# Second branch's output projection: the last pair of heads last for three feature tiles, two of them held behind the last head's values, the fourth on a score bank

## The chip, the cores and the metric

The kernel runs on one core of a Trainium2 chip. The time is that of one execution on the device, in microseconds; the median of several runs counts. The engines are TensorE (PE, matrix products, with its weight loads PEld), VectorE (DVE), ScalarE (ACT), GpSimd (POOL) and SyncE (SP, which issues most DMAs). Each works through its own instructions in the order of its program; waits between engines are semaphores. Products land in PSUM, eight banks of 128 x 512 float32.

## What is computed

One layer of an encoder over 512 frames of width 1024, in float32:

```python
hn = rms_norm(x, norm1_g[l])
proj = hn @ w_in[l]                       # q, k, v of branches A and B, gates A and B
out_a = chunked_attention(qa, ka, va, ...)      # 8 heads x 64, softmax
out_b = stick_breaking_attention(qb, kb, vb)    # 8 heads x 64, no softmax
mixed = (sigmoid(gate_a) * (out_a @ w_branch_a[l])
         + sigmoid(gate_b) * (out_b @ w_branch_b[l]))
x = x + mixed @ w_out[l]
x = x + conv_glu(rms_norm(x, norm2_g[l]), ...)
```

The change concerns `out_b @ w_branch_b[l]`, a product of 512 x 512 by 512 x 1024.

## The kernel before

Every float32 product is made of three: both operands are split into a rounded high part and the rest (`hi`, `lo`), and `mm3` issues high by high (L312), high by rest (L313) and rest by high (L314) into one bank. A step of the contraction (128 wide) is thus three products, each with a stationary 128 x 128 block and 512 moving columns. In `mm3` for the second branch the stationary operand is the weight (`whi_yB`, `wlo_yB`) and the moving one the heads' output (`oh_B`, `ol_B`).

The weights come in chunks in a fixed order; the ones here are `gB3` (gates), `yB0` and `yB1` (the two halves of `w_branch_b`, four feature tiles each) and `wo0` to `wo3`. `run_chunk` runs a chunk's body, and between the body's yields it emits the casts of the next chunk (`split_gen`: L281 on ACT for the high part, L286 on DVE for the rest).

The attention heads run in steps. For the last head of branch B, `trans` transposes the weights of the attention (L770) and splits them (L783 on ACT into `pth_B`, L784 on DVE into `ptl_B`), and `pv` multiplies them with the values (L793, eight products, 512, 384, 256 and 128 columns wide, each for `pth` and `ptl`). Its result is put together over ACT (L800, `ot_B`) and DVE (L801, `of_B`) and split again: `oh_B` (L805, ACT) and `ol_B` (L806, DVE). Two heads make one pair, 128 rows; `ots["B"]` holds the four pairs, and the contraction of the output projection runs over them, `k` 0 to 3. Pair 3 is complete only after the last head's `pv`.

`yB_body` uses `feat_groups`: for each feature tile one bank, and in it the four pairs in order. The evacuation of a tile multiplies by the gate (`gb`, L882), adds to the first branch's part (`mixA`, L883), and splits into `mh` (L889, ACT) and `ml` (L890, DVE). After each tile the loop around it emits two pieces of `park`, background work that has nothing to do with this stage: blocks of the later up-projection are summed (`pkr`, L203, DVE), split (L208 ACT, L209 DVE) and stored by DMA.

What is written is an order of emission. A planner then orders each engine's instructions: it takes ready instructions by priority, by its own model of costs, and hands out buffers from the pools; `tc.high_priority` raises the priority (as around `trans` and `pv`), and `park` lowers it. An emission order is thus a wish and not the final one; `behind(ins, others)` adds an order between two instructions without a semaphore. On chip each engine's order is fixed.

The PSUM banks are handed out by tag:

```python
SC = lambda n: ptile("sc", 2, n)     # two banks, scores
TR = lambda n: ptile("tr", 2, n)     # two banks, transposes
PV = lambda n: ptile("pv", 1, n)     # one bank, attention times values
MM = lambda n: ptile("mm", 3, n)     # three banks, projections
```

and the loops that use them here are

```python
def feat_groups(hi, lo, name, n, kn, mh, ml, evac):
    for j in range(n):
        ps = MM(f"{name}_{j}")
        for k in range(kn):
            cs = slice(j * P, (j + 1) * P)
            mm3(ps, hi[:, k, cs], lo[:, k, cs], mh(k), ml(k), k == 0, k == kn - 1)
```

After yB1 the output projection `wo` takes its banks in turn from SC, TR, PV and MM.

Of the kernel before, what the change touches and what calls it, by code (L numbers as in the profile page):

```python
# [15 lines left out]
P = 128  # L16
S = 512
D = 1024
NT = S // P
# [56 lines left out]
def block_kernel(ctx: ExitStack, tc: tile.TileContext, x, xt, params, g2, rbx, wts, wd0, wd1, out):  # L76
    nc = tc.nc
    V, A, G, PE, SP = nc.vector, nc.scalar, nc.gpsimd, nc.tensor, nc.sync
# [230 lines left out]

    def mm3(ps, sh, sl, mh, ml, first, last):  # L310

        PE.matmul(ps, sh, mh, start=first, stop=False)  # L312
        PE.matmul(ps, sh, ml, start=False, stop=False)  # L313
        PE.matmul(ps, sl, mh, start=False, stop=last)  # L314


    hth = hp.tile([P, NK, S], F32R, tag="hth", name="hth")
# [15 lines left out]
    def ptile(tag, bufs, name):  # L333
        return pp.tile([P, S], F32, tag=tag, name=name, bufs=bufs)

    SC = lambda n: ptile("sc", 2, n)
    TR = lambda n: ptile("tr", 2, n)
    PV = lambda n: ptile("pv", 1, n)
    MM = lambda n: ptile("mm", 3, n)
# [21 lines left out]
    for i in range(WARM):  # L361
        PE.matmul(pw.rearrange("p (a b) -> p a b", a=4), warm, warm.unsqueeze(1).to_broadcast([P, 4, P]),
                  start=True, stop=True)
# [139 lines left out]
    def tok_groups(hi, lo, name, evac):  # L503
        for tp in range(2):
            ps = MM(f"{name}_{tp}")
            for j in range(2):
                t = 2 * tp + j
                o = ps[:, j * 256:(j + 1) * 256]
                for k in range(NK):
                    ts_ = slice(t * P, (t + 1) * P)  # L510
                    mm3(o, hth[:, k, ts_], htl[:, k, ts_], hi[:, k, :], lo[:, k, :], k == 0, k == NK - 1)
                if j == 1:
                    evac(tp, ps)
                yield
# [78 lines left out]
# [6 lines that stand above are left out]
                if kn == 8 and k == 3:  # L599
                    yield  # L600
            evac(j, ps)
            yield
# [131 lines left out]
    def behind(ins, others):  # L734

        for o in others:
            tc.add_manual_dep(ins.ins, o.ins.name, mybir.DependencyInfo(
                mybir.DependencyClass.NoSync, mybir.DependencyReason.DATA), reason="table order")
        return ins
# [46 lines left out]
    def pv(br, h):  # L786
        ph, pl = pts.pop((br, h))
        vt = vts[f"v{br}{h // 4}"]
        ps = PV(f"pv_{br}{h}")
        for k in range(NT):  # L790
            o, n = OFF[k] + k * P, S - k * P
            for j, src in enumerate((ph, pl)):
                PE.matmul(ps[:, k * P:], vt[:, k, h % 4, :], src[:, o:o + n],  # L793
                          start=(k == 0 and j == 0), stop=(k == NT - 1 and j == 1))
        i = h % 2
        if i == 0:
            pv.o = pool_o.tile([P, S], F32, tag="of", name=f"of_{br}{h}", bufs=1)
        tmp = pool_wk.tile([P, S], F32, tag="wb", name=f"ot_{br}{h}", bufs=5)
        own, oth = ((LO, HI), (HI, LO))[i]
        A.copy(tmp[own, :], ps[oth, :])  # L800
        V.tensor_tensor(pv.o[own, :], ps[own, :], tmp[own, :], op=ALU.add)  # L801
        if i == 1:
            oh = pool_o.tile([P, S], F32R, tag="oh", name=f"oh_{br}{h}", bufs=4)
            ol = pool_o.tile([P, S], F32R, tag="ol", name=f"ol_{br}{h}", bufs=4)
            A.copy(oh, pv.o)  # L805
            V.tensor_tensor(ol, pv.o, oh.bitcast(F32), op=ALU.subtract)  # L806
            ots[br].append((oh, ol))
# [44 lines left out]
    for s in range(len(steps)):  # L852
        if s + LA < len(steps):
            start_step(s + LA)
        target = n_groups * (s + 1) / (len(steps) + 6)
        while emitted < target:
            next(fg, None)
            emitted += 1
        if 14 <= s < 56:
            park()  # L860
        br, h, t, e = pend.pop(0)
        with tc.high_priority(HP):
            trans(br, h, t, e)
        if t == NT - 1:
            if (br, h) in need_v:
                fill_until(need_v[br, h])
            with tc.high_priority(HP):
                pv(br, h)
# [5 lines left out]
    def yB_body(i):  # L874
        def body(hi, lo):
            o = ots["B"]
            m = mix["t"]

            def evac(j, ps):
                f = 4 * i + j  # L880
                g = gbs[f]
                V.tensor_tensor(g, ps, g, op=ALU.mult)  # L882
                V.tensor_tensor(m[:, f, :], g, m[:, f, :], op=ALU.add)  # L883
                if f % 4 == 0:
                    mxt["h"] = pool_v.tile([P, 4, S], F32R, tag="v", name=f"mh{f}", bufs=2)
                if f % 2 == 0:
                    mxt["l"] = pool_pt.tile([P, 2, S], F32R, tag=("pth", "ptl")[f // 2 % 2], name=f"ml{f}", bufs=2)
                mh, ml = mxt["h"][:, f % 4, :], mxt["l"][:, f % 2, :]
                A.copy(mh, m[:, f, :])  # L889
                V.tensor_tensor(ml, m[:, f, :], mh.bitcast(F32), op=ALU.subtract)  # L890
                mxs.append((mh, ml))
            yield from feat_groups(hi, lo, f"yB{i}", 4, 4, lambda k: o[k][0], lambda k: o[k][1], evac)
        return body

    n = 0
# [22 lines left out]
    def rows_group(prefix, banks, src, n, fin, c, t, hi, lo):  # L918

        for hf in range(2):  # L920
            if c == 0:
                banks[t, hf] = BANK(f"{prefix}_{t}{hf}", t // 2)
            ps = banks[t, hf]
            for kk in range(2):
                sh, sl = src[2 * c + kk]
                ts_, cs = slice(t * P, (t + 1) * P), slice(hf * 512, (hf + 1) * 512)
                mm3(ps, sh[:, ts_], sl[:, ts_], hi[:, kk, cs], lo[:, kk, cs],
                    c == 0 and kk == 0, c == n - 1 and kk == 1)
            if c == n - 1:
                fin(t, hf, ps)  # L930
            yield
# [31 lines left out]
    hi, lo = splits.pop("wo3")  # L963
# [448 lines left out]
```

## Time and profile before

| | us |
|---|---|
| median of 3 runs (range) | 720.12 (719.87 to 720.14) |
| the profiled execution | 719.62 |
| its span, first to last instruction | 717.9 |
| PE busy | 711.6 |
| DVE busy | 588.6 |
| ACT busy | 410.0 |
| POOL busy | 55.2 |
| granted TensorE clock, mean | 1.00 |

Times in the trace count from the start of the span. The stage of the change lies at about 309 to 328 us. In a timeline a row is the start, the duration, the engine, the line, the operation, output and inputs by tile name (buffer numbers left out), and in brackets the idle time ahead of it and what ended it; in the list of waits the three numbers are the total, the number of times and the longest. In a row by stretches the engines' busy times stand behind the stretch's length, then the granted clock and the DMA figures.

### The profile page before, as it was taken

The page shows a single profiled execution, that of the slowest core. Times are in us where ns is not written, and L with a number is a line of the kernel's source. Part 1 is how long each engine was busy: PE and PEld are TensorE (multiplying, and loading weights), DVE is VectorE, ACT ScalarE, POOL GpSimd, SP SyncE. Part 2 cuts the span into 40 slices and gives each one's busy share as a digit, 9 for nine tenths or more (in the row PEclk, how much of TensorE's full clock was granted, in tenths as well). Part 3 has the DMA queues.
Part 4 walks back from the last instruction along what each step waited for, and adds up shares of the span by engine and source line. Part 5 has one row for each costly group of instructions (what it writes and reads, how often), then busy time and mean ns, then how long its engine had stood idle before and what let it go on. Part 6 is the DMA issues. An engine that isn't in the chain of part 4 may idle for free.

```text
span 717.9 us, 10814 instructions
## 1 busy us (share of the span) xinstructions
PE 711.6 (99%) x3983; PEld 619.6 (86%) x3983; DVE 588.6 (82%) x1051; ACT 410.0 (57%) x756; POOL 55.2 (8%) x91
## 2 busy tenths in 40 slices
PE   9999999999999999999999999999999999999997
PEld 7889998888988888878889988999988988888886
DVE  6678878786998998869556698999999985997687
ACT  6576657667776677544335564656655543543531
POOL 2501200000110111100003000000000100000000
PEclk9999999999999999999999999999999999999999
DMA  9722236435344444554937837667665633564563
GB/s 315 290 75 89 89 118 204 164 132 205 137 162 142 180 159 159 199 184 162 336 127 284 270 112 280 231 235 284 246 249 205 230 132 113 187 247 167 179 213 117
DMA packets 38613, 136.59 MB, mean 190 GB/s; under 512 B 4128, under 2 KB 8864, under 8 KB 31008
## 3 DMA queue, kind: packets, MB, share of 16 engines
q1 hardware_dynamic: 35616, 122.66, 47.9%
q0 software_dynamic: 2656, 13.11, 4.9%
q8 instruction: 31, 0.51, 0.3%
q14 instruction: 22, 0.18, 0.1%
q10 hardware_dynamic: 288, 0.14, 0.1%
HBM read 109.41 MB, written 26.48 MB: 189 GB/s over the span
## 4 chain that ended last, share of the span: by engine, by line
PE 97%; DVE 2%; ACT 0%; issue 0%; DVEq 0%; ACTq 0%
PE P L1245 15%; PE p L1151 12%; PE pg L313 3%; PE pg L312 3%; PE pg L314 3%; PE pu L313 3%; PE pu L314 3%; PE pu L312 3%; PE vA L443 3%; PE uA L443 3%; PE qkB L314 2%; PE gB L312 2%; PE qkB L312 2%; PE qkB L313 2%; PE gB L313 2%; PE gB L314 2%
## 5 line engine op out<-in xcount | busy, mean ns | idle before, releaser
L1245 PE MATMUL P<-whi_dn,ax 128*128 128x512 f32 x176 | 54.3, 389 | 0.0
L166 ACT CAST whi_dn<-raw_dn 128x1024 fp32r<-128x1024 f32 x33 | 34.3, 1051 | 25.8 <-PE P L1245 16.5
L162 DVE TENSOR_TENSOR wlo_dn<-raw_dn,whi_dn 128x1024 fp32r<-128x1024 f32 x33 | 40.0, 1223 | 9.5 <-ACT whi_dn L166 9.5
L314 PE MATMUL pg<-hth,wlo_up 128*128 128x512 f32 (+1 forms) x120 | 43.3, 361 | 0.0
L312 PE MATMUL pg<-hth,whi_up 128*128 128x512 f32 (+1 forms) x120 | 43.2, 361 | 0.0
L313 PE MATMUL pg<-htl,whi_up 128*128 128x512 f32 (+1 forms) x120 | 43.2, 360 | 0.0
L313 PE MATMUL pu<-htl,whi_up 128*128 128x512 f32 (+1 forms) x116 | 41.6, 359 | 0.0
L312 PE MATMUL pu<-hth,whi_up 128*128 128x512 f32 (+1 forms) x116 | 41.6, 359 | 0.0
L314 PE MATMUL pu<-hth,wlo_up 128*128 128x512 f32 (+1 forms) x116 | 41.6, 358 | 0.0
L1245 PE MATMUL P<-whi_dn,ay 128*128 128x512 f32 x132 | 40.8, 389 | 0.0
L1245 PEld LDWEIGHTS P<-whi_dn,ax 128*128 128x128 f32 x176 | 33.0, 188 | 6.8
L208 ACT CAST pkh<-pkr 128x512 fp32r<-128x512 f32 x24 | 14.9, 621 | 36.5 <-DMA parked<-pkh 15.3
L286 DVE TENSOR_TENSOR wlo_up<-raw_up,whi_up 128x1024 fp32r<-128x1024 f32 (+1 forms) x32 | 31.3, 1019 | 4.9 <-ACT whi_up L281 4.9
L1245 PE MATMUL P<-wlo_dn,ax 128*128 128x512 f32 x88 | 34.2, 389 | 0.0
L281 ACT CAST whi_up<-raw_up 128x1024 fp32r<-128x1024 f32 (+1 forms) x32 | 26.5, 886 | 10.9 <-PE pu L313 6.1
L754 POOL TENSOR_SCALAR_AFFINE_SELECT bB<-bB 128x128 f32<-128x128 f32 x32 | 18.7, 592 | 151.4 <-DVE bB L753 149.3
L1245 PEld LDWEIGHTS P<-whi_dn,ay 128*128 128x128 f32 x132 | 24.8, 188 | 5.1
L752 DVE TENSOR_TENSOR_SCAN aB<-aB,reset 128x127 f32<-128x127 f32 (+3 forms) x32 | 25.7, 813 | 4.1 <-ACT aB L747 4.1
L209 DVE TENSOR_TENSOR pkr<-pkr,pkh 128x512 fp32r<-128x512 f32 x24 | 16.4, 684 | 12.4 <-ACT pkh L208 12.4
L1245 PE MATMUL P<-wlo_dn,ay 128*128 128x512 f32 x66 | 25.8, 391 | 0.0
L312 PE MATMUL gA<-hth,whi_gA 128*128 128x512 f32 x64 | 25.5, 399 | 0.3 <-DVE mixA L632 0.3
L1151 PE MATMUL p<-ts,whi_up 128*128 128x256 f32 x144 | 25.5, 277 | 0.0
(324 smaller groups left out, 2397.6 us busy)
## 6 DMA issues: line engine op xcount, KB each, us to landing
raw_up<-in_wts SPq DMA_DIRECT2D x14, 1024.0 KB, 5.4
raw_dn<-in_wd SPq DMA_DIRECT2D x11, 1024.0 KB, 4.8
pkr<-in_wts SPq DMA_DIRECT2D x8, 1024.0 KB, 6.8
parked<-pkr SPq DMA_DIRECT2D x32, 256.0 KB, 2.5
parked<-pkh SPq DMA_DIRECT2D x24, 256.0 KB, 2.1
raw_dn<-in_wd SPq DMA_DIRECT2D x11, 512.0 KB, 3.3
ayd<-ay POOLq DMA_DIRECT2D x7, 768.0 KB, 6.3
ay<-ayd POOLq DMA_DIRECT2D x7, 768.0 KB, 6.1
```

Of the source, the lines that this page charges most:

```text
L162: chain("halves", V.tensor_tensor(o, x, y, op=op))
L166: chain("casts", A.copy(hi[:, sl], src))
L281: A.copy(hi[:, sl], raw[:, sl])
L286: V.tensor_tensor(lo[:, sl], raw[:, sl], hi[:, sl].bitcast(F32), op=ALU.subtract)
L312: PE.matmul(ps, sh, mh, start=first, stop=False)
L313: PE.matmul(ps, sh, ml, start=False, stop=False)
L314: PE.matmul(ps, sl, mh, start=False, stop=last)
L443: PE.matmul(pss[t], st[:, 4 * half + k, t * P:(t + 1) * P], mv[:, k, :], start=half == 0 and k == 0 and j == 0, stop=half == 1 and k == 3 ...
L752: V.tensor_tensor_scan(ar, ar, reset[:, S - n:S - 1][:, ::-1], 1.0, op0=ALU.mult, op1=ALU.max)
L754: G.affine_select(b[:, n - P:n], b[:, n - P:n], pattern=[[-1, P]], compare_op=ALU.is_gt, fill=0.0, base=0, channel_multiplier=1)
L1151: PE.matmul(ps, st, mv[:, k, :], start=first and k == 0 and n == 0, stop=last and k == 3 and n == 2, skip_group_check=True)
L1245: chain("products", PE.matmul(dst, st, mv, start=first and n == 0, stop=last and n == 2, skip_group_check=True))
```

## The change

`mm3` returns its first instruction, and `pv` keeps its last one. For `yB0` the loop is written out: three tiles take MM banks; for each the first three pairs are emitted, then for each the last pair with the evacuation; then the fourth tile in one piece, on an SC bank. The first products of tiles 1 and 2 are ordered behind the last product of `pv`. `yB1` is as before. The yields stay four, one behind each tile's evacuation.

```diff
     def mm3(ps, sh, sl, mh, ml, first, last):
 
-        PE.matmul(ps, sh, mh, start=first, stop=False)
+        ins = PE.matmul(ps, sh, mh, start=first, stop=False)
         PE.matmul(ps, sh, ml, start=False, stop=False)
         PE.matmul(ps, sl, mh, start=False, stop=last)
+        return ins
...
             for j, src in enumerate((ph, pl)):
-                PE.matmul(ps[:, k * P:], vt[:, k, h % 4, :], src[:, o:o + n],
-                          start=(k == 0 and j == 0), stop=(k == NT - 1 and j == 1))
+                pv.last = [PE.matmul(ps[:, k * P:], vt[:, k, h % 4, :], src[:, o:o + n],
+                                     start=(k == 0 and j == 0), stop=(k == NT - 1 and j == 1))]
...
-            yield from feat_groups(hi, lo, f"yB{i}", 4, 4, lambda k: o[k][0], lambda k: o[k][1], evac)
+            if i == 1:
+                yield from feat_groups(hi, lo, "yB1", 4, 4, lambda k: o[k][0], lambda k: o[k][1], evac)
+                return
+            pss = [MM(f"yB0_{j}") for j in range(3)]
+            for j, ks in [(j, (0, 1, 2)) for j in range(3)] + [(j, (3,)) for j in range(3)] + [(3, range(4))]:
+                if j == 3:
+                    pss.append(SC("yB0_3"))
+                cs = slice(j * P, (j + 1) * P)
+                for k in ks:
+                    ins = mm3(pss[j], hi[:, k, cs], lo[:, k, cs], *o[k], k == 0, k == 3)
+                    if k == 0 and j in (1, 2):
+                        behind(ins, pv.last)
+                if 3 in ks:
+                    evac(j, pss[j])
+                    yield
```

## The prediction

> **What bounds the kernel now.** First the page, for the shares of the engines and the chain that ended last; then the list of waits of TensorE; then the timeline around the second branch's output projection.
>
> ```profile
> span 717.9 us, 10814 instructions
> PE 711.6 (99%) x3983; PEld 619.6 (86%) x3983; DVE 588.6 (82%) x1051; ACT 410.0 (57%) x756; POOL 55.2 (8%) x91
> PE 97%; DVE 2%; ACT 0%; issue 0%; DVEq 0%; ACTq 0%
> ```
>
> TensorE (PE) is busy for 99% of the span and makes up 97% of the chain that ended last. So time can be won only where PE stands still or steps slowly. The list of waits, for PE alone and over the whole span, has four entries:
>
> ```profile
> PE warm L362 <- DVE warm L359: 1.1, 1, 1.1
> PE yB L313 <- DVE ol_B L806: 0.4, 1, 0.4
> PE gA L312 <- DVE mixA L632: 0.3, 1, 0.3
> PE yB L312 <- DVE gb L882: 0.3, 1, 0.3
> ```
>
> Two of the four lie in yB, the tile that the change touches. PE's timeline there:
>
> ```profile
> 306.94 0.60 PE L770 MATMUL pT_B<-ident,bB 128*128 128x128 f32 x4
> ...
> 309.00 0.39 PE L312 MATMUL yB<-oh_B,whi_yB 128*128 128x512 f32 x1
> ...
> 312.42 0.39 PE L793 MATMUL pv_B<-pth_B,v_vB 128*128 128x512 f32 x1
> 312.64 0.39 PE L312 MATMUL yB<-oh_B,whi_yB 128*128 128x512 f32 x1
> ...
> 313.10 0.39 PE L793 MATMUL pv_B<-ptl_B,v_vB 128*128 128x512 f32 x1
> ...
> 314.08 0.44 PE L314 MATMUL yB<-oh_B,wlo_yB 128*128 128x512 f32 x1
> 314.36 0.39 PE L312 MATMUL yB<-oh_B,whi_yB 128*128 128x512 f32 x1
> ...
> 316.43 0.89 PE L312 MATMUL yB<-oh_B,whi_yB 128*128 128x512 f32 x3
> 317.75 0.50 PE L313 MATMUL yB<-ol_B,whi_yB 128*128 128x512 f32 x1 [0.43 <-DVE ol_B L806]
> 318.09 0.39 PE L314 MATMUL yB<-oh_B,wlo_yB 128*128 128x512 f32 x1
> ...
> 319.01 0.40 PE L314 MATMUL yB<-oh_B,wlo_yB 128*128 128x512 f32 x1
> 319.67 0.50 PE L312 MATMUL yB<-oh_B,whi_yB 128*128 128x512 f32 x1 [0.26 <-DVE gb L882]
> 320.01 0.40 PE L313 MATMUL yB<-ol_B,whi_yB 128*128 128x512 f32 x1
> ...
> 322.52 0.39 PE L312 MATMUL yB<-oh_B,whi_yB 128*128 128x512 f32 x1
> ...
> 327.74 0.39 PE L314 MATMUL yB<-oh_B,wlo_yB 128*128 128x512 f32 x1
> ```
>
> Each row is a start and a modelled duration; the durations overlap, so the step from start to start is what counts. From 322.52 to 327.74 lie 24 products without a wait: 5.22 over 23 steps, 0.227 us a step. yB0 and yB1 share the name yB, but the order on PE is visible: 17 yB products (15 from 309.00 and two from 312.64) stand ahead of the bulk of the eight pv products, ten from 314.08 behind them. 27 is three feature tiles with three pairs of heads each. Then come three L312 products with the last pair's oh, and PE stands until ol_B is made. Then six more, and PE stands again until DVE has emptied a bank (gb, L882) for the fourth tile.
>
> **The change part by part.** Nothing is added or removed: 48 yB0 products, eight pv products, the same evacuations, casts, parks and DMAs. Only the order and one bank move.
>
> *The size of the stall.* From 316.43 to 318.09 PE makes four steps in 1.66 us; at 0.227 they take 0.91, so 0.75 is lost at the wait for ol_B. From 319.01 to 320.01 it makes two steps in 1.00, against 0.45, so 0.55 is lost at the bank. Together 1.30 us; the list's 0.4 and 0.3 are less, since the refill of the pipeline is lost too. I take 1.27, the rounding of the starts being against me. [...]
>
> *The holding (tiles 1 and 2 behind the last pv product).* It is an order on one engine, without a semaphore, and costs no instruction. Eighteen products then stand behind pv instead of ten. Ahead of pv remain tile 0's nine, and tile 3's nine, since its bank (a score bank) is free: the last head's scores are consumed by then, as the transposes of what is made from them run at 306.94. If the planner puts tile 3 there, as it has put whatever was ready there so far, pv starts where it does now, 312.42, and ends as now at 314.08. If it doesn't, pv comes right behind tile 0's nine, near 311.05; its operands allow that, by the first two rows here:
>
> ```profile
> 308.68 0.27 ACT L783 CAST pth_B<-pT_B 128x128 fp32r<-128x128 f32 x1 [0.62 <-DVE ptl_B L784]
> 308.98 0.29 DVE L784 TENSOR_TENSOR ptl_B<-pT_B,pth_B 128x128 fp32r<-128x128 f32 x1 [0.33 <-ACT pth_B L783]
> 309.81 2.49 DVE L286 TENSOR_TENSOR wlo_yB<-raw_yB,whi_yB 128x512 fp32r<-128x512 f32 x4
> 311.70 1.28 ACT L909 ACT_TABLE_LOAD   x1
> 314.33 0.58 ACT L800 COPY ot_B<-pv_B 64x512 f32<-64x512 f32 x1 [1.35 <-PE pv_B L793]
> 314.94 0.69 DVE L801 TENSOR_TENSOR of_B<-pv_B,ot_B 64x512 f32<-64x512 f32 x1 [2.04 <-ACT ot_B L800]
> 315.67 1.42 DVE L203 TENSOR_TENSOR pkr<-pkr 128x512 f32<-128x512 f32 x2
> 317.01 0.69 DVE L806 TENSOR_TENSOR ol_B<-of_B,oh_B 128x512 fp32r<-128x512 f32 x1
> 317.61 0.69 DVE L203 TENSOR_TENSOR pkr<-pkr 128x512 f32<-128x512 f32 x1
> 318.21 0.69 DVE L209 TENSOR_TENSOR pkr<-pkr,pkh 128x512 fp32r<-128x512 f32 x1
> ```
>
> *The last pair last.* With pv as now, the eighteen held products run from 314.08: 0.28 for the first step, 17 at 0.227, so tile 0's first product with oh starts at 318.22 and its first with ol at 318.45. ol_B is made at 317.01 + 0.69 = 317.70. The cover is 0.75 us. Without tile 3 ahead, pv ends some 1.4 us sooner, near 312.3, and the chain of values with it, but the table load holds ACT to 312.98. From pv's end at 314.08 to 317.70 the chain takes 3.62, two pkr pieces included; begun at 312.98 it would end at 316.6, against a product due near 316.6. So 0 to 0.1 us of a stall there at most, and I take the cover of the first order.
>
> *The fourth tile on a score bank.* The bank wait, 0.55 us, goes: tile 3 has a bank from the start. The next that needs an evacuated bank is yB1's first tile, 13 products behind 318.22, at 321.17. Tile 0 closes at 318.22 + 2 × 0.227 + 0.39 = 319.06; the wait for DVE and gb itself then take, by the next fence, 0.60 to 0.70, so the bank is free near 319.95. Cover 1.2 us, two DVE instructions.
>
> *What follows on DVE.* No instruction moves between queues. SP gets no new issue, and the parks (pkr pieces, their DMAs) are as many, two behind each finished tile. But DVE runs without a gap from 318.93 on, so the four tiles, closed within 2.7 us, are evacuated at DVE's pace:
>
> ```profile
> 319.00:336.00 17.00, 16.74 (x74) 13.54 (x73) 16.34 (x27) 7.43 (x13) 0.00 (x0) 1.00 0.49 164
> 318.93 1.89 DVE L882 TENSOR_TENSOR gb<-yB,gb 128x512 f32<-128x512 f32 x3
> 324.94 1.89 DVE L286 TENSOR_TENSOR wlo_wo<-raw_wo,whi_wo 128x512 fp32r<-128x512 f32 x3
> 327.35 0.69 DVE L286 TENSOR_TENSOR wlo_wo<-raw_wo,whi_wo 128x512 fp32r<-128x512 f32 x1
> 331.59 0.39 PE L313 MATMUL wo<-wlo_wo,mh 128*128 128x512 f32 x1
> 347.00:717.90 370.90, 366.72 (x2103) 321.97 (x2101) 300.17 (x446) 185.67 (x281) 14.35 (x26) 1.00 0.59 210
> ```
>
> The first row gives, behind the length, PE, weight loads, DVE (16.34 of 17.00 us), ACT and POOL. The nearest consumer at risk is the first product with wlo_wo, at 331.59; its operand is done at 328.04. Cover 3.55 now, and 2.28 when PE comes 1.27 sooner, still three to four DVE instructions of 0.60. The late stages have PE without a wait in the list, so I cost what follows at nothing and expect the gain to reach the end.
>
> *Sum.* The profiled execution took 719.62 (span 717.9 and 1.72 around it), 0.50 under the median. 719.62 − 1.27 = 718.35 for an execution like it; 720.12 − 1.27 = **718.85** for the median. This is 0.18%. About 0.2% (1.44 us) is what a measurement of this kernel can tell from no change, so the whole gain falls just under it. It can't be much over: no other stall is touched, and even the whole stretch from 309.00 to 322.52 (13.52) against 48 × 0.227 + 1.20 for pv (0.22 for the first, 0.98 from 313.10 to 314.08) would give 1.42.
>
> **The rivals.**
> *Part of the stall stays.* The planner, not the program, places the pkr pieces, and two already stood ahead of ol_B. One more (0.60) is within the cover of 0.75; two more leave 0.45, three 1.05: 719.3 to 719.9. For it: the new order of emission puts parks at other places. Against: they have the lowest priority.
> *The stall moves and nothing is won:* 720.1. pv is the gate of everything behind it now. Were pth and ptl made behind the weight casts (wlo_yB, 2.49) instead of ahead of them, pv would start its second product about 1.3 us later than tile 0's nine end, and the gain would be gone. That they are ahead today speaks against it. A change that does not do what it says (tiles 1 and 2 still ahead of pv) would give the same 720.1.
> *Slower, by one mechanism:* DVE's backlog reaches wlo_wo. From four more DVE instructions ahead of its last piece PE waits; from six (3.6 − 2.28 = 1.3) the gain is spent; with nine, 5.4 − 2.28 = 3.1 is lost, 718.85 + 3.1 = 722.0. For it: DVE has no gap there. Against: of the four tiles' twelve evacuation instructions ten (gb 4, mixA 4, ml 2 between 318.93 and 327.35) stood ahead of it already, so seven would have to be parks.
> *Slower steps from alternating banks.* PE now goes round four banks while short of work. The kernel's start shows what slow steps cost:
>
> ```profile
> 1.12 4.21 PE L362 MATMUL warm<-warm 128*128 128x512 f32 x9 [1.12 <-DVE warm L359]
> 5.13 1.23 PE L449 MATMUL uA<-whi_uA,hth 128*128 128x256 f32 x8
> ```
>
> Nine products in 4.01 us, 0.446 each, 0.22 over the later step; nine such would cost 2.0 and give 720.8. Against: PE already alternated three banks at 316.43 and stood twice, and the 12 steps from 319.67 to 322.52 still took 0.24 each, refill included, with the clock at 1.00 in the stretch above. [...]
>
> **How the numbers follow.** Full removal 0.68 (its own range 718.5 to 719.2; 0.11 of it past 0.2%, through the spread of runs, 719.87 to 720.14, and the 1.42 bound); part of it 0.13; nothing won 0.11; DVE backlog or a like stall further on 0.07, of which 0.06 past 0.2%; slow steps 0.01. So faster 0.11, within 0.2% 0.83, slower 0.06. The range runs from 718.5 to 720.3: it takes in the partial case and no gain, and leaves out about 0.14.
>
> **What would show it.** Right: the list of PE's waits has no yB row left; behind the last pv product 18 or 19 products run at 0.227 before the first with the last pair; yB1's first product starts near 321.2 instead of 322.52, and wo's first correspondingly sooner. Wrong: a wait for ol_B or gb still there (first rival), a wait of pv_B for pth or ptl (second), a wait of wo for wlo_wo or ml (third), or fewer than 18 products behind pv.

## The result, and the profile after

The changed kernel takes 718.87 us (median of 15 runs, 718.12 to 720.05) against 720.14 (15 runs, 719.57 to 720.89): a ratio of 0.9982, 95% interval 0.9974 to 0.9990. That is 1.27 us less. It is under the 0.2% (1.44 us) that the prediction takes as the least that a measurement can tell from no change, but the interval excludes 1.

The list of PE's waits over the whole span, after:

```profile
PE warm L363 <- DVE warm L360: 1.1, 1, 1.1
PE uA L450 <- ACT whi_uA L281: 0.5, 1, 0.5
PE gA L312 <- DVE mixA L633: 0.3, 1, 0.3
```

Both yB rows are gone. The uA row is new and has nothing to do with the change: it is a wait for the first weights, at the start, and the same kernel run once more (below) doesn't have it. PE's timeline of the stage, after:

```profile
309.63 0.39 PE L312 MATMUL yB<-oh_B,whi_yB 128*128 128x512 f32 x1
...
313.04 0.39 PE L794 MATMUL pv_B<-pth_B,v_vB 128*128 128x512 f32 x1
...
314.59 0.27 PE L794 MATMUL pv_B<-ptl_B,v_vB 128*128 128x128 f32 x1
314.70 0.44 PE L312 MATMUL yB<-oh_B,whi_yB 128*128 128x512 f32 x1
...
318.64 0.62 PE L314 MATMUL yB<-oh_B,wlo_yB 128*128 128x512 f32 x2
319.09 1.07 PE L312 MATMUL yB<-oh_B,whi_yB 128*128 128x512 f32 x4
320.00 0.39 PE L313 MATMUL yB<-ol_B,whi_yB 128*128 128x512 f32 x1
320.22 0.39 PE L314 MATMUL yB<-oh_B,wlo_yB 128*128 128x512 f32 x1
...
321.81 0.39 PE L312 MATMUL yB<-oh_B,whi_yB 128*128 128x512 f32 x1
...
330.20 0.39 PE L313 MATMUL wo<-wlo_wo,mh 128*128 128x512 f32 x1
```

There are no brackets left: nothing waits. pv starts 3.41 us behind yB's first product, as before (312.42 − 309.00). Here and below, differences are taken from the trace's nanoseconds, so they can be 0.01 off those of the rounded rows. 19 products stand behind it instead of ten, then four L312 products with the last pair (the x4 row: all four tiles have a bank), and only then the first with ol, at 320.00.

For the experiments I use one measure from the trace, the *stretch* from yB's first product to yB1's first, the 49th: before 322.52 − 309.00 = 13.52, after 321.81 − 309.63 = 12.19, so 1.33 less. What lies behind the stretch is 395.4 us in both (717.9 − 322.52 and 717.2 − 321.81). So the whole gain is in these 13 us, and all of it is kept to the end. The two profiled spans differ by only 0.7, since the profiled run after came to the stage 0.62 later: the start varies from run to run (308.98 and 310.43 in two of the runs below), the stretch hardly (12.19 in both profiles of the changed kernel).

DVE, after:

```profile
312.84 0.69 DVE L203 TENSOR_TENSOR pkr<-pkr 128x512 f32<-128x512 f32 x1
315.56 0.69 DVE L802 TENSOR_TENSOR of_B<-pv_B,ot_B 64x512 f32<-64x512 f32 x1 [2.04 <-ACT ot_B L801]
316.29 1.42 DVE L203 TENSOR_TENSOR pkr<-pkr 128x512 f32<-128x512 f32 x2
317.63 0.69 DVE L807 TENSOR_TENSOR ol_B<-of_B,oh_B 128x512 fp32r<-128x512 f32 x1
...
320.65 1.29 DVE L883 TENSOR_TENSOR gb<-yB,gb 128x512 f32<-128x512 f32 x2 [1.13 <-PE yB L314]
...
327.26 0.69 DVE L286 TENSOR_TENSOR wlo_wo<-raw_wo,whi_wo 128x512 fp32r<-128x512 f32 x1
```

ol_B is made no sooner: two pkr pieces are ahead of it as before, and it is done at 318.31. It is PE that comes for it later, at 320.00.

### The profile page after: what moved, and what is told of

It is laid out like the page before. It is cut to its first block, busy times and chain, and to the rows that moved or that the text cites. A ratio compares the mean times of both kernels' runs of the same rounds, so it can differ in the third digit from the quotient of the medians.

```text
span 717.2 us, 10812 instructions
## 1 busy us (share of the span) xinstructions
PE 711.0 (99%) x3983; PEld 619.6 (86%) x3983; DVE 588.8 (82%) x1051; ACT 409.6 (57%) x756; POOL 55.1 (8%) x91
## 4 chain that ended last, share of the span: by engine, by line
PE 97%; DVE 1%; DMA 1%; ACT 0%; issue 0%; SPq 0%; DVEq 0%
PE P L1260 15%; PE p L1166 12%; PE pg L314 3%; PE pg L313 3%; PE pg L312 3%; PE pu L314 3%; PE pu L313 3%; PE pu L312 3%; PE vA L444 3%; PE uA L444 3%; PE qkB L314 2%; PE gB L312 2%; PE qkB L312 2%; PE qkB L313 2%; PE gB L313 2%; PE gB L314 2%
## 5 line engine op out<-in xcount | busy, mean ns | idle before, releaser
L312 PE MATMUL pg<-hth,whi_up 128*128 128x512 f32 (+1 forms) x120 | 43.2, 361 | 0.0
L312 PE MATMUL pu<-hth,whi_up 128*128 128x512 f32 (+1 forms) x116 | 41.6, 359 | 0.0
L312 PE MATMUL gA<-hth,whi_gA 128*128 128x512 f32 x64 | 25.5, 399 | 0.3 <-DVE mixA L633 0.3
L312 PE MATMUL gB<-hth,whi_gB 128*128 128x512 f32 x64 | 25.4, 397 | 0.0
```

The source lines that it names most:

```text
L312: ins = PE.matmul(ps, sh, mh, start=first, stop=False)
```

## The experiments

**Taking the change apart.** The changed kernel once more, then three versions with a part taken away, and one with a single part.

| kernel | order written out | hold | fourth tile's bank | stretch | time | ratio to before (95%) |
|---|---|---|---|---|---|---|
| before | no | no | projection | 13.52 | 720.15 | |
| changed | yes | yes | score | 12.19 | 718.76 | 0.9978 (0.9969 to 0.9987) |
| no hold | yes | no | score | 12.19 | 719.02 | 0.9984 (0.9975 to 0.9993) |
| hold, no score bank | yes | yes | projection | 12.91 | 719.83 | 0.9997 (0.9988 to 1.0006) |
| order alone | yes | no | projection | 13.52 | 721.06, one run | |
| score bank alone | no | no | score | 12.19 | 718.89 | 0.9982 (0.9973 to 0.9991) |

The last row comes from a later chip session, where before took 720.03. The single run of "order alone" reached yB only at 310.43, 1.43 later than the profile before: its time tells nothing, its stretch does. Each stretch is that of one profile.

The changed kernel again:

> The changed kernel as it is, beside the others on one chip. Theory (the 1.27 us of waiting in yB0 is all that goes): 1.2 to 1.4 us under before, about 718.9; from yB's first product to yB1's first 12.2 us, against 13.5 before. Rival (part of the difference between the two profiled runs is something else, such as the start): the stretch differs by less than 1 us.

12.19 and 718.76: as the theory.

Without the hold:

```diff
-                    if k == 0 and j in (1, 2):
-                        behind(ins, pv.last)
```

> Emission order and score bank kept, the order behind the last pv product taken away. Theory A (the score bank gives the cover; the hold decides only which tiles' products stand ahead of pv): 17 yB products ahead of pv's end as now, then 10 of tiles 1 and 2 and nine of tile 3, so again 19 behind pv; no wait left in yB, 12.2 us for the stretch, 718.9. Rival B (the hold gives the cover by moving products behind pv): a wait for ol_B of about 0.4 is back, 719.6 or more.

Theory A. The stretch is the same to 0.01 us and no yB wait is in the list.

Hold kept, score bank taken away:

```diff
-                    pss.append(SC("yB0_3"))
+                    pss.append(MM("yB0_3"))
```

> Emission order and hold kept, the fourth tile on one of the three projection banks. Theory A: only tile 0's nine stand ahead of pv, pv runs near 2 us after yB's first product instead of 3.4, eighteen products behind it cover ol_B, so the wait for ol_B (0.75 with its refill) goes, and the bank wait (0.55) stays in whole or in part: stretch 12.4 to 12.8 us, 719.2 to 719.6. Rival B (both waits need the bank): the stretch stays near 13.5, 720.1.

Theory A in kind: the wait for ol_B is gone and one for the bank is left. PE's list of waits and the rows around it:

```profile
PE yB L312 <- DVE gb L883: 0.4, 1, 0.4
```

```profile
311.03 0.39 PE L794 MATMUL pv_B<-pth_B,v_vB 128*128 128x512 f32 x1
...
318.21 0.39 PE L314 MATMUL yB<-oh_B,wlo_yB 128*128 128x512 f32 x1
...
319.03 0.50 PE L312 MATMUL yB<-oh_B,whi_yB 128*128 128x512 f32 x1 [0.43 <-DVE gb L883]
319.37 0.39 PE L313 MATMUL yB<-ol_B,whi_yB 128*128 128x512 f32 x1
```

pv starts 2.05 us behind yB's first product (308.98), right behind tile 0's nine, so the hold does what it says. But the two steps from 318.21 to 319.37 take 1.16 instead of 0.45: the bank costs 0.70 here, not 0.55, the stretch is just above the expected 12.8, and the time of 719.83 is above the expected 719.6. Its interval includes 1, so what the hold is worth without the score bank is seen in the stretch alone.

Order alone:

> Emission order alone: no hold, fourth tile on a projection bank. Theory A (the planner had already put the last pair last): nothing changes, waits for ol_B 0.4 and for gb 0.3 as before, stretch 13.5 us. Rival B (the written-out order is what removes the waits): stretch 12.2 to 12.8 us.

Theory A: both waits are back, 0.4 for ol_B and 0.3 for gb, and the stretch is that of before.

Score bank alone, one edit to the kernel before:

```diff
-            ps = MM(f"{name}_{j}")
+            ps = (SC if name == "yB0" and j == 3 else MM)(f"{name}_{j}")
```

> The kernel before with one edit: the fourth tile of yB0 on a score bank; the loop, its emission order and the lack of a hold as before. Theory A (a bank that is free at once is all that the change needs; the planner does the rest): no wait in yB, stretch from yB's first product to yB1's first 12.2 us, time as the changed kernel, near 718.9. Rival B (the order of emission has a part): a wait for ol_B or gb is left, stretch 12.5 us or more.

Theory A. PE's rows have the same shape as after the whole change:

```profile
314.52 0.27 PE L793 MATMUL pv_B<-ptl_B,v_vB 128*128 128x128 f32 x1
314.63 0.44 PE L314 MATMUL yB<-oh_B,wlo_yB 128*128 128x512 f32 x1
...
319.02 1.07 PE L312 MATMUL yB<-oh_B,whi_yB 128*128 128x512 f32 x4
319.93 0.39 PE L313 MATMUL yB<-ol_B,whi_yB 128*128 128x512 f32 x1
```

One bank that is free at once removes both waits: the bank wait directly, and the wait for ol_B because the fourth tile's nine products with the first three pairs can be put ahead of the last pair. With the hold or without, 17 products stand ahead of pv's end and 19 behind it; the hold only decides which tiles they belong to.

**What made ol_B late.** The kernel before, with three parked block sums ordered behind the last ol_B:

```diff
+    sums = []
...
-                V.tensor_tensor(b[o], b[x], b[y], op=op)
+                sums.append(V.tensor_tensor(b[o], b[x], b[y], op=op))
...
-            V.tensor_tensor(ol, pv.o, oh.bitcast(F32), op=ALU.subtract)
+            ins = V.tensor_tensor(ol, pv.o, oh.bitcast(F32), op=ALU.subtract)
+            if (br, h) == ("B", 7):
+                for p in sums[-3:]:
+                    behind(p, [ins])
```

> The kernel before, with the last three block sums of the parked work (pkr, L203) that are emitted before the last pair ordered behind ol_B; no hold, no score bank. Theory A (two pkr pieces on DVE ahead of ol_B made the first wait): ol_B is made 0.6 to 1.3 us sooner after pv, the wait for ol_B goes, and the bank wait stays in part: stretch from yB's first product to yB1's first 12.3 to 13.0 us, 719.0 to 719.7. Rival B (the wait is pv's place, not DVE's order): the wait for ol_B stays at 0.4 and the stretch at 13.5.

The stretch is in theory A's range: 12.69, no wait for ol_B, 0.2 left for the bank, and no pkr row ahead of ol_B. DVE:

```profile
314.43 0.69 DVE L803 TENSOR_TENSOR of_B<-pv_B,ot_B 64x512 f32<-64x512 f32 x1 [1.73 <-ACT ot_B L802]
315.81 0.69 DVE L808 TENSOR_TENSOR ol_B<-of_B,oh_B 128x512 fp32r<-128x512 f32 x1 [0.69 <-ACT oh_B L807]
```

ol_B is done 3.05 us behind the start of pv's last product (313.45), against 3.72 before. But the planner moved pv too: it starts 2.49 us behind yB's first product instead of 3.41, and 14 products stand behind it instead of ten. Before, ol_B came 0.59 us late (317.70 against 317.11, three steps behind 316.43). The 0.68 won on DVE would cover that, and so would the four products (0.91), so this run does not show which of them took the wait away. The run with the hold and no score bank has two pkr pieces ahead of ol_B and no wait for it: pv's place alone can suffice.

The kernel takes 724.53 us against 720.52 (ratio 1.0055, interval 1.0041 to 1.0069), where 719.0 to 719.7 was expected. The profiled execution is the slowest of five, 726.25. Its loss against the profile before lies behind the stretch, 402.45 instead of 395.4, and 3.7 of these 7 us are waits that the kernel before doesn't have:

```profile
PE p L1156 <- DVE cg L994: 1.8, 1, 1.8
PE pg L316 <- DVE wlo_up L288: 1.4, 1, 1.4
PE p L1156 <- DVE wlo_up L255: 0.5, 1, 0.5
```

Holding the parked work here pushes it into the later stages: between 347 and 400, 14 parked instructions start on DVE, against one before, and it is busy for 32.36 us, against 28.32. Between 400 and 500, where these three waits lie, the mean granted clock is 0.98, against 1.00 before (last section). Whether the parked work makes all of the 7 us was not tested.

**How much cover there is.** The last ol_B is written over several times, with the same result, so that the products with ol have more DVE work ahead of them. Each of these kernels was run once, so the stretch is read and not the time.

```diff
+            for _ in range(3 if (br, h) == ("B", 7) else 1):
+                V.tensor_tensor(ol, pv.o, oh.bitcast(F32), op=ALU.subtract)
```

Changed kernel, three times over:

> The changed kernel with the last ol_B written three times over (the same subtraction, twice more), so two DVE instructions more ahead of the last pair's products with ol. In the changed kernel's profile ol_B is made at 318.3 and first used at 320.0: a cover of 1.7 us. Theory A (cover 1.7; parks slip in between the repeats): two repeats and the parks between them are 1.2 to 2.4 us, so a wait of 0 to 0.7 plus refill; stretch 12.2 to 13.1 us. Rival B (the cover is the 0.75 of the prediction): a wait of 0.5 to 1.6, stretch 12.8 to 14.0 us.

ol_B is done 11.22 us behind yB's first product instead of 8.69 (318.31 − 309.63), 2.54 later; the stretch is 13.27, 1.09 longer. A cover of 1.69 (320.00 − 318.31) leaves 0.85; the other 0.24 is near the 0.32 and 0.29 that the two waits in the kernel before lost beyond their listed length (0.75 − 0.43 and 0.55 − 0.26). With 0.75 it would have been 1.79 at least. Both ranges held the result; the size decides for A.

Five times over:

> The changed kernel with the last ol_B written five times over (four more DVE instructions of 0.6, parks between them). Theory A: with the cover of 1.7 us the wait for ol_B grows by about 1.2 to 2.4 us over the run with two repeats; stretch 13.5 to 15.5 us, and the time grows by the same. Rival B (the wait is hidden again, by other products put in its place): stretch under 13 us.

15.82, a little over the upper end of A: no other products are put in its place. The wait for ol_B is 3.12 us.

Kernel before, three times over:

> The kernel before with the last ol_B written three times over. Theory A (no cover there): each added DVE instruction up to the last ol_B, parks between them too, costs in full: 1.2 to 2.4 us more, stretch 14.7 to 15.9 us, wait for ol_B 1.6 to 2.8. Rival B: the bank wait behind it absorbs part, stretch under 14.5 us.

The wait for ol_B is 3.0, and the stretch 16.86, 3.34 longer for 2.53 of delay: more than A allows. The reason is in the steps behind the stall; see the last section.

Changed kernel, twice over:

> The changed kernel with the last ol_B written twice over; two pkr pieces come between, so three DVE instructions more (1.8 us) ahead of the products with ol. Theory (cover of 1.69, shown by the run with ol_B three times over: 2.54 later, 1.08 lost): 1.8 - 1.69 = 0.1, with the refill up to 0.3; stretch 12.2 to 12.5 us.

The first half came true and the stretch did not: 13.23. The step to the first product with ol takes 0.41, 0.18 over the usual. But then:

```profile
319.28 1.07 PE L312 MATMUL yB<-oh_B,whi_yB 128*128 128x512 f32 x4
320.37 0.50 PE L313 MATMUL yB<-ol_B,whi_yB 128*128 128x512 f32 x1
...
322.09 0.39 PE L314 MATMUL yB<-oh_B,wlo_yB 128*128 128x512 f32 x1
323.05 0.50 PE L312 MATMUL yB<-oh_B,whi_yB 128*128 128x512 f32 x1 [0.57 <-DVE gb L884]
```

```profile
319.63 0.68 DVE L808 TENSOR_TENSOR ol_B<-of_B,oh_B 128x512 fp32r<-128x512 f32 x1
321.58 0.69 DVE L209 TENSOR_TENSOR pkr<-pkr,pkh 128x512 fp32r<-128x512 f32 x1 [1.26 <-ACT pkh L208]
322.30 2.48 DVE L884 TENSOR_TENSOR gb<-yB,gb 128x512 f32<-128x512 f32 x4
```

A parked piece that itself waits 1.26 us for ACT stands ahead of the evacuation, and yB1's first tile waits for its bank. In the changed kernel as it is, that piece stands behind the first two evacuations (321.86), so the added write has moved the planner's order too. In this run the bank for yB1 is what costs most, and not ol_B.

Kernel before, twice over:

> The kernel before with the last ol_B written twice over, three DVE instructions (1.8 us) more. With ol_B three times over, 2.5 us more of delay cost 3.34, and the products after the stall stepped at 0.43. Theory A (PE's steps are slow only after a stall of about 3 us; this one is about 2.4): the delay costs 1.8 and no more, steps of 0.23 behind it, stretch 15.1 to 15.5 us. Rival B (the slow steps follow shorter stalls too): stretch 16 us or more.

16.34: theory A failed, rival B holds for this kernel.

## Why the prediction was right

*The size of the stall:* predicted 1.27, measured 1.33 in the stretch (13.52 to 12.19) and 1.27 in the medians. *The whole gain reaches the end:* 395.4 us behind the stretch in both. *The bound of 1.42* held.

*pv as now, tile 3 ahead:* right, 3.41 us behind the first product in both.

*The holding.* Here the attribution was wrong, and the sum did not show it. The step credited the eighteen products behind pv to the hold, and the bank wait to the score bank. The runs without the hold and with the score bank alone have the same 12.19: the hold adds nothing once the fourth tile has its own bank. That the sum came out right is thus in part luck: two waits were given to two parts of the change, and one part removes both. The hold is worth 0.61 (12.91 against 13.52) only without that bank. The written order is worth nothing by itself; the planner had it already, as the 27 products ahead of the first wait showed.

*The last pair last:* cover predicted 0.75, measured 1.69. I let tile 0's three closing products come first; the planner put a 19th product and the L312 of all four tiles ahead of the first with ol, 0.9 us more. The ol_B runs confirm 1.69.

*The fourth tile on a score bank:* the bank for yB1 was to be free near 319.95 with a cover of 1.2. It was free at 321.34 (320.65 + 0.69) for a product at 321.81: 0.47. The same order is the cause: tile 0's last product starts at 320.22, and not at 319.30 (318.67 and the 0.62 by which the stage came later). Of the three covers measured here it is the thinnest.

*What follows on DVE:* cover for wlo_wo predicted 2.28; done at 327.95, used at 330.20: 2.25. That agreement is luck: counted from yB's first product, both came 0.7 us sooner than predicted. Nor did wo's first product come sooner, as the signs had it: it starts at 329.97 instead of 327.96, since the planner put it behind 36 products of yB1 instead of 24.

*The rivals.* Nothing stayed, moved or slowed in the changed kernel. "The stall moves" is what the twice-over run shows, at the yB1 bank, not at pv. The slow steps did not come with four banks (12 steps of 0.227 from 319.09 to 321.81, the clock at 1.00), but they do come behind some stalls: 0.43 behind waits of 2.23 and 2.95 us (last section).

## What to carry to other kernels

When an engine waits for a late operand and its planner reorders, look first for products that could run but have no bank: one free bank from another pool can be worth more than an order written by hand. Test each part of a change alone, since a sum that comes out right doesn't show which part earned it. Follow the cover to the next link (here the bank for yB1, 0.47 us), and don't hold back background work in one place without looking where it lands.

## What was not expected of the hardware

Behind a stall of 2.23 us on PE the steps were slow, and behind a longer one, of 3.12, they were not. In the kernel before with ol_B twice over, by stretches and in the timeline:

```profile
316.00:320.00 4.00, 1.77 (x8) 1.06 (x7) 3.71 (x6) 0.55 (x1) 0.00 (x0) 0.99 0.96 325
320.00:324.00 4.00, 4.00 (x11) 3.01 (x12) 3.20 (x6) 1.24 (x2) 0.00 (x0) 0.59 0.53 204
```

```profile
319.80 0.73 PE L313 MATMUL yB<-ol_B,whi_yB 128*128 128x512 f32 x1 [2.23 <-DVE ol_B L807]
320.33 0.63 PE L314 MATMUL yB<-oh_B,wlo_yB 128*128 128x512 f32 x1
320.75 0.63 PE L313 MATMUL yB<-ol_B,whi_yB 128*128 128x512 f32 x1
```

The granted clock falls to 0.59 in the four microseconds behind a wait of 2.23, and the step is 0.43 instead of 0.227 for seven steps: 1.4 us on top of the stall. With ol_B three times over (a wait of 2.95) five steps are slow, at 0.43, and the clock is 0.57 from 320 to 324; behind the changed kernel's shorter stall with ol_B three times over (0.7) none is. But behind the longest stall, in the changed kernel with ol_B five times over, the clock stays at 1.00 and the steps at 0.23 to 0.24, once the first is over:

```profile
320.00:324.00 4.00, 0.88 (x4) 0.63 (x4) 2.82 (x6) 1.24 (x2) 0.00 (x0) 1.00 0.61 234
324.00:328.00 4.00, 3.97 (x18) 2.90 (x17) 3.94 (x7) 1.85 (x4) 0.00 (x0) 1.00 0.45 147
```

```profile
323.27 0.50 PE L313 MATMUL yB<-ol_B,whi_yB 128*128 128x512 f32 x1 [3.12 <-DVE ol_B L808]
323.62 0.40 PE L314 MATMUL yB<-oh_B,wlo_yB 128*128 128x512 f32 x1
```

So the length of a wait alone does not decide: the steps are slow behind 2.23 and 2.95 us, and not behind 3.12. In the run with the parked sums held the clock falls too, to a mean of 0.98 between 400 and 500, where waits of 1.8, 1.4 and 0.5 lie. What decides was not shown: no run was made to test it. So the wait of 2.23 us cost 1.4 more than its length through the slow steps, and the two that the change removed, 0.43 and 0.26, had no slow steps behind them and cost 0.75 and 0.55.
